# Eight gate products emitted ahead of the layer norm that follows the convolution

## The chip, the cores and the metric

The kernel runs on one core of one Trainium2 chip. The metric is the device time of one execution in microseconds (us); of several runs the median is compared.

## The reference, cut to what matters

Three transformer blocks follow one another over 512 tokens of width 1024. The change lies in the first. Its convolution branch gates a product, convolves it over 31 taps, normalizes the result over the channels and projects it; a second gate, `g_conv`, is a product of the block's normed input `h` with 1024 columns of `w_in` and needs nothing of the convolution:

```python
(q, kc, vc, ks_, vs_, kw, vw, g_nsa, u_a, u_b, g_attn, g_conv) = jnp.split(rms_norm(x) @ w_in, ...)
z = u_a * sigmoid(u_b)
z = depthwise_conv(z, conv_w) + conv_b                    # 31 taps
zn = (z - mean(z)) * rsqrt(var(z) + EPS) * ln_g + ln_b    # over the channels
conv = silu(zn) @ w_conv_out + b_conv_out
merged = sigmoid(g_attn) * attn + sigmoid(g_conv) * conv
x = x + merged @ w_out
```

## The kernel before, in words

All activations lie transposed in SBUF: 8 tiles of 128 channels by 512 tokens (`X[:, k]`, k = 0 to 7). A product ("gemm", L165 to L174) makes one 128x512 tile of its result: it takes a weight unit of 128x1024, which SP's queue loads into one of two raw buffers (`wst`), ACT rounds in two halves to `wh` (L155) and POOL completes with the rest `wl` (L156); `wh` and `wl` have four half-unit buffers each, so two units. TensorE (PE) then runs 24 matmuls, for each of 8 input tiles one each of L171, L172 and L173, into one PSUM bank (`pg`). The eviction of the gates is done by `proj` (L675 to L683): DVE multiplies `pg` by the root-mean-square factor `R` (L680).

The convolution of a channel tile is 30 DVE instructions over one PSUM bank `py` (L673), with ACT's first tap ahead of them (L671) and ACT's copy into `X[:, c]` behind them (L674). They are emitted in the attention stage, but with their place put back by 3000:

```python
with tc.high_priority(offset=-LOW):      # LOW = 3000
    y = K.ps("y")
```

The order of instructions on each engine is not the order of the source. A planner (the Tile scheduler) lays it out before the kernel runs: it reckons through the program with costs of its own, and whenever an engine is free in that reckoning it takes, of the instructions that it reckons ready, the one emitted first. What stands on an engine's list is then executed in that order, whatever becomes ready earlier on the chip; a list's head that waits holds up all behind it. The planner also reckons when a buffer is free. Behind the attention stage the PSUM pool is closed and a new one of eight banks is opened (`K.psum(g=5, m=3)`): five banks for products, three for column sums.

After that come, in this order of emission:

- `norm.feed(k)`, k = 0 to 7 (L286 to L303): a first column sum on PE over tiles 0 and 1 (`colsum`, L198, one fp32 matmul with a matrix of ones, two rows in the trace) gives `c`, which ACT copies (L295); DVE subtracts `c` from each tile (L306), ACT squares it (L314), DVE adds up sums and squares (L277).
- at k = 7 `finish` (L317 to L333): two more column sums, mean `mu` (L321), variance, then `newton` (L212 to L224): a preload of an ACT table (L209), Ln (L216), Exp (L217), three DVE steps that end with `r` (L224). While they go on, `mu` is subtracted, four tiles on DVE and four on POOL (L331).
- the eight gate products: `proj(I["w1_gc"][m])` and ACT's tanh into `gc` (L1015).
- for each tile: multiply by `r` (DVE L336), ACT affine (L1021), ACT tanh (L1023), DVE L1024, and the split into two operands `zn` (DVE L193, L194).
- the eight products of the convolution branch's projection, which read `zn` (`w1_co`), each ended by ACT L1030 and DVE L1031, L1032 (with `gc` and the attention) and the split `mg`; then the eight products of `w_out`, which read `mg`.

Of the kernel before, what the change touches and what calls it, by code (L numbers as in the profile page):

```python
# [21 lines left out]
NT = 8  # L22
# [568 lines left out]
def block1(K, X, entry):  # L591
# [84 lines left out]
    def proj(w, scale=None, out=None):  # L676
        ps = K.gemm(K.gps(), gx, w if isinstance(w, list) else K.wunit(w))
        s = K.tmp() if out is None else out
        if scale is None:
            nc.vector.tensor_tensor(s, ps, R, MUL)  # L680
        else:
            nc.vector.scalar_tensor_tensor(s, ps, scale, R, op0=MUL, op1=MUL)
        return s  # L683
# [323 lines left out]
    sC = ExitStack()  # L1007
    norm = Norm(0, K, X, 1e-6, sC)
    pC = sC.enter_context(tc.tile_pool(name="b1d", reuse_waits="tile", bufs=16))
    for k in range(NT):  # L1010
        norm.feed(k)
    sgc = []
    for m in range(NT):
        sgc.append(pC.tile([P, T], F32, tag="gc", bufs=8, name=K.nm("gc")))
        nc.scalar.activation(sgc[m], proj(I["w1_gc"][m]), AF.Tanh, scale=0.5)  # L1015
    zn = []
    alloc = lambda tag: (lambda: pC.tile([P, T], F32R, tag=tag, name=K.nm(tag)))
    for k in range(NT):
# [1016 lines left out]
def program(tc, I, out, first=1, last=3):  # L2035
    with ExitStack() as es:
# [7 lines left out]
        if first == 1:  # L2044
            block1(K, X, entry)
        else:
            tc.nc.sync.dma_start(X, I["x_in"].rearrange("(c p) t -> p c t", p=P))
            K.psum(g=5, m=3)
# [36 lines left out]
```

## Time and profile before

| | us |
|---|---|
| median of 3 runs | 2914.58 (2907.49 to 2914.98) |
| the profiled execution | 2904.16 |
| its span in the trace | 2902.4 |

The span runs from the first to the last instruction that the profiler recorded; the rest of the profiled execution, 1.8 us, lies around it. All times of the trace are counted from the span's start. The stage that the change touches lies at 487 to 620 us.

### The profile page before, as it was taken

The numbers are of one execution on the slowest core, as the hardware profiler recorded it, in microseconds if no ns is written. First come the engines' busy times: TensorE is split into PE (matmuls) and PEld (weight loads), VectorE is DVE, ScalarE is ACT, GpSimd is POOL, SyncE is SP. The second block draws the span as 40 slices with busy tenths as digits, with TensorE's granted clock in tenths as the row PEclk, the third lists the DMA queues.
The fourth block names the chain that finished last, engine by engine and source line by source line (L and its number), as shares of the span: only waits on it lengthen the run. The fifth ranks groups of instructions, "written<-read, shape, count | busy, mean of one in ns | idle before, by whom it ended". The sixth has DMA issues, their size and how long they took to land.

```text
span 2902.4 us, 34153 instructions
## 1 busy us (share of the span) xinstructions
PE 2676.3 (92%) x12206; PEld 2120.0 (73%) x12206; DVE 1780.9 (61%) x2825; ACT 1283.2 (44%) x2317; POOL 1306.6 (45%) x1023
## 2 busy tenths in 40 slices
PE   7899999699999988988889999999988889999997
PEld 5677776478888856766676788877766678788885
DVE  7889899965243596776774821126877765422246
ACT  4357875533222354444443533332556652322234
POOL 6554432554444454333332644454544344444443
PEclk9999999799999999999999999999999899999999
DMA  3321111232322222222222222232222122222223
GB/s 115 114 86 54 54 38 37 77 105 91 98 95 94 95 67 96 70 78 73 70 70 68 67 101 95 95 116 88 94 89 75 49 80 87 92 98 95 95 95 102
DMA packets 79193, 243.32 MB, mean 84 GB/s; under 512 B 11312, under 2 KB 15320, under 8 KB 79024
## 3 DMA queue, kind: packets, MB, share of 16 engines
q1 hardware_dynamic: 79024, 241.15, 25.3%
q8 instruction: 96, 1.57, 0.2%
q14 instruction: 73, 0.60, 0.1%
HBM read 230.96 MB, written 4.52 MB: 81 GB/s over the span
## 4 chain that ended last, share of the span: by engine, by line
PE 63%; DVE 23%; ACT 6%; DMA 3%; issue 3%; POOL 2%; SPq 0%; DVEq 0%; ACTq 0%; POOLq 0%
PE pg L172 18%; PE pg L173 18%; PE pg L171 18%; DMA B<-diag 2%; DVE p L1894 1%; DVE py L673 1%; DVE X L336 1%; DVE QK L1310 1%; PE ppt L956 1%; POOL wl L156 1%; DMA diag<-dg 1%; DVE ln L277 1%; DVE Zt L1416 1%; PE ps L934 1%; DVE Z L1417 1%
## 5 line engine op out<-in xcount | busy, mean ns | idle before, releaser
L156 POOL TENSOR_TENSOR wl<-wst,wh 128x512 fp32r<-128x512 f32 (+1 forms) x808 | 1099.9, 1367 | 1367.1 <-ACT wh L155 1285.7
L155 ACT ACTIVATE wh<-wst 128x512 fp32r<-128x512 f32 (+1 forms) x808 | 500.8, 627 | 1102.1 <-PE pg L172 918.1
L171 PE MATMUL pg<-op,wh 128*128 128x512 f32 (+1 forms) x2008 | 812.7, 405 | 38.9 <-ACT wh L155 19.5
L172 PE MATMUL pg<-op,wh 128*128 128x512 f32 (+1 forms) x2008 | 808.6, 403 | 2.6 <-DVE op L191 2.4
L173 PE MATMUL pg<-op,wl 128*128 128x512 f32 (+1 forms) x2008 | 807.2, 402 | 3.9 <-POOL wl L156 3.9
L171 PEld LDWEIGHTS pg<-op,wh 128*128 128x128 f32 (+1 forms) x2008 | 386.7, 193 | 120.9 <-ACT wh L155 20.1
L173 PEld LDWEIGHTS pg<-op,wl 128*128 128x128 f32 (+1 forms) x2008 | 386.2, 192 | 83.6 <-POOL wl L156 6.7
L172 PEld LDWEIGHTS pg<-op,wh 128*128 128x128 f32 (+1 forms) x2008 | 387.3, 193 | 82.2 <-DVE op L191 5.8
L171 PE MATMUL pg<-hid,wh 128*128 128x512 f32 x688 | 272.2, 396 | 0.9 <-DVE hid L190 0.9
L173 PE MATMUL pg<-hid,wl 128*128 128x512 f32 x688 | 272.1, 396 | 0.0
L172 PE MATMUL pg<-hid,wh 128*128 128x512 f32 x688 | 271.8, 395 | 0.2 <-DVE hid L191 0.2
L673 DVE SCALAR_TENSOR_TENSOR py<-z,vec,py 128x512 f32<-128x512 f32 x240 | 180.2, 751 | 10.9 <-ACT py L671 6.2
L1120 DVE TENSOR_TENSOR X<-X,pg 128x512 f32<-128x512 f32 x56 | 38.5, 688 | 222.1 <-PE pg L173 222.1
L171 PEld LDWEIGHTS pg<-hid,wh 128*128 128x128 f32 x688 | 129.2, 188 | 32.9 <-DVE hid L190 1.3
L172 PEld LDWEIGHTS pg<-hid,wh 128*128 128x128 f32 x688 | 129.2, 188 | 31.9 <-DVE hid L191 0.5
L173 PEld LDWEIGHTS pg<-hid,wl 128*128 128x128 f32 x688 | 129.2, 188 | 31.3 <-issue 0.2
L190 DVE CAST hid<-t 128x512 fp32r<-128x512 f32 x86 | 53.0, 616 | 145.7 <-ACT t L1097 145.0
L1111 DVE SCALAR_TENSOR_TENSOR t<-pg,R 128x512 f32<-128x512 f32 x32 | 22.1, 691 | 84.0 <-PE pg L173 83.9
L938 ACT ACTIVATE P<-ps,s 128x128 f32<-128x128 f32 (+3 forms) x128 | 66.4, 523 | 11.6 <-DVE s L937 9.5
L191 DVE TENSOR_TENSOR hid<-t,hid 128x512 fp32r<-128x512 f32 x86 | 63.6, 740 | 3.0
L937 DVE TENSOR_REDUCE s<-ps 128x1 f32<-128x128 f32 (+3 forms) x128 | 60.1, 483 | 8.1 <-PE ps L936 6.6
L960 DVE TENSOR_TENSOR PTl<-ppt,PTh 128x512 fp32r<-128x512 f32 x80 | 53.4, 684 | 4.7 <-ACT PTh L959 3.9
(523 smaller groups left out, 4344.3 us busy)
## 6 DMA issues: line engine op xcount, KB each, us to landing
wst<-in_w_f_dram SPq DMA_DIRECT2D x64, 512.0 KB
wst<-in_w_up_dram SPq DMA_DIRECT2D x32, 512.0 KB
wst<-in_w_down_dram SPq DMA_DIRECT2D x32, 512.0 KB
wst<-in_w_ga_dram SPq DMA_DIRECT2D x24, 512.0 KB
wst<-in_w_fg_dram SPq DMA_DIRECT2D x22, 512.0 KB
wst<-in_w_fu_dram SPq DMA_DIRECT2D x22, 512.0 KB
wst<-in_w_q_dram SPq DMA_DIRECT2D x16, 512.0 KB
wst<-in_w_out_dram SPq DMA_DIRECT2D x16, 512.0 KB
```

Source lines behind the costliest of these rows:

```text
L155: nc.scalar.activation(h, st, AF.Copy)
L156: nc.gpsimd.tensor_tensor(l, st, h, SUB)
L171: self.nc.tensor.matmul(ps, lhsT=wh, rhs=h[:, sl], start=first and k == 0, stop=False)
L172: self.nc.tensor.matmul(ps, lhsT=wh, rhs=l[:, sl], start=False, stop=False)
L173: self.nc.tensor.matmul(ps, lhsT=wl, rhs=h[:, sl], start=False, stop=last and k == n - 1)
L190: nc.vector.tensor_copy(h, src)
L191: nc.vector.tensor_tensor(l, src, h, SUB)
L673: nc.vector.scalar_tensor_tensor(y, z[:, k:k + T], w(k), y, op0=MUL, op1=ADD)
L937: nc.vector.tensor_reduce(mx[:, h:h + 1], S[:, :L], AX, MAX, negate=True)
L938: nc.scalar.activation(Pt[h][:, :L], S[:, :L], AF.Exp, bias=mx[:, h:h + 1], accum_out=den[:, h:h + 1])
L960: nc.vector.tensor_tensor(tl, pt, th, SUB)
L1120: nc.vector.tensor_tensor(X[:, m], X[:, m], ps, ADD)
```

## The change

The loop that feeds the layer norm and the loop that emits the eight gate products trade places. No instruction is added, removed or altered; a product's loads, roundings, matmuls, eviction and tanh move with it.

```diff
     norm = Norm(0, K, X, 1e-6, sC)
     pC = sC.enter_context(tc.tile_pool(name="b1d", reuse_waits="tile", bufs=16))
-    for k in range(NT):
-        norm.feed(k)
+
     sgc = []
     for m in range(NT):
         sgc.append(pC.tile([P, T], F32, tag="gc", bufs=8, name=K.nm("gc")))
         nc.scalar.activation(sgc[m], proj(I["w1_gc"][m]), AF.Tanh, scale=0.5)
+    for k in range(NT):
+        norm.feed(k)
     zn = []
```

## Rows read from the trace of the kernel before

**Rows 1.** The page's head: span, and PE's busy time, share and instructions.
```profile
span 2902.4 us, 34153 instructions
PE 2676.3 (92%) x12206; PEld 2120.0 (73%) x12206; DVE 1780.9 (61%) x2825; ACT 1283.2 (44%) x2317; POOL 1306.6 (45%) x1023
```
**Rows 2.** Stretches of the stage: length, busy us of each engine, clock, DMA share, GB/s.
```profile
487.10:504.30 17.20, 14.82 (x51) 11.07 (x50) 14.95 (x22) 1.97 (x3) 0.00 (x0) 0.80 0.03 10
504.30:523.10 18.80, 0.06 (x2) 0.04 (x1) 17.01 (x25) 2.93 (x6) 0.01 (x1) 0.63 0.00 0
523.10:537.70 14.60, 7.36 (x14) 3.88 (x14) 13.64 (x20) 5.52 (x10) 10.32 (x4) 0.50 0.11 36
537.70:573.90 36.20, 33.97 (x138) 27.04 (x137) 34.54 (x40) 26.61 (x39) 23.81 (x15) 0.92 0.33 103
573.90:620.30 46.40, 46.34 (x199) 37.01 (x198) 34.49 (x38) 16.85 (x28) 25.20 (x18) 1.00 0.37 125
```
**Rows 3.** Timeline of PE: start, length, line, operation, idle time before and its releaser.
```profile
489.49 2.05 PE L198 MATMUL pm<-ln,ones 128*128 128x512 f32 x2 [2.38 <-DVE ln L292]
...
490.55 1.42 PE L171 MATMUL pg<-op,wh 128*128 128x512 f32 x1
...
503.94 0.39 PE L173 MATMUL pg<-op,wl 128*128 128x512 f32 x1
523.06 0.79 PE L171 MATMUL pg<-op,wh 128*128 128x512 f32 x1 [18.74 <-ACT wh L155]
...
524.82 0.80 PE L173 MATMUL pg<-op,wl 128*128 128x512 f32 x1 [0.54 <-POOL wl L156]
...
534.88 3.78 PE L198 MATMUL pm<-ln,ones 128*128 128x512 f32 x4 [6.71 <-DVE ln L277]
...
573.89 0.40 PE L171 MATMUL pg<-zn,wh 128*128 128x512 f32 x1
...
619.01 0.40 PE L171 MATMUL pg<-mg,wh 128*128 128x512 f32 x1
...
997.92 1.12 PE L198 MATMUL pm<-ln,ones 128*128 128x512 f32 x2
```
**Rows 4.** Timeline of ACT around the end of the convolution.
```profile
518.81 0.60 ACT L674 ACTIVATE X<-py 128x512 f32<-128x512 f32 x1 [23.78 <-DVE py L673]
519.31 0.59 ACT L295 ACTIVATE c<-pm 128x512 f32<-128x512 f32 x1
...
522.40 0.61 ACT L155 ACTIVATE wh<-wst 128x512 fp32r<-128x512 f32 x1
```
**Rows 5.** Timeline of DVE.
```profile
484.60 0.68 DVE L680 TENSOR_TENSOR t<-pg,R 128x512 f32<-128x512 f32 x1
...
535.36 0.68 DVE L680 TENSOR_TENSOR t<-pg,R 128x512 f32<-128x512 f32 x1
...
549.89 8.02 DVE L336 TENSOR_TENSOR X<-X,r 128x512 f32<-128x512 f32 x6
...
561.06 0.68 DVE L336 TENSOR_TENSOR X<-X,r 128x512 f32<-128x512 f32 x1
561.66 0.68 DVE L194 SCALAR_TENSOR_TENSOR zn<-X,zn 128x512 fp32r<-128x512 f32 x1
562.26 0.41 DVE L193 TENSOR_SCALAR zn<-X 128x512 fp32r<-128x512 f32 x1
...
577.52 1.67 DVE L194 SCALAR_TENSOR_TENSOR zn<-X,zn 128x512 fp32r<-128x512 f32 x1
```
**Rows 6.** Timeline of ACT: table loads before Ln and Exp; below, the next norm.
```profile
542.80 1.28 ACT L216 ACT_TABLE_LOAD   x1 [1.16 <-DVE ln L326]
544.10 0.63 ACT L216 ACTIVATE ln<-ln 128x512 f32<-128x512 f32 x1
...
545.27 1.28 ACT L217 ACT_TABLE_LOAD   x1
...
1046.04 0.63 ACT L217 ACTIVATE r<-ln 128x512 f32<-128x512 f32 x1
```

## The prediction

> **What bounds the kernel now.** The page's head first: PE is busy 92% of the span [rows 1], so most of the kernel pays for a stall only where PE itself stalls. The table of stretches then shows where this stage is different: from 504.3 to 523.1 us PE does next to nothing while DVE is busy 17.0 of 18.8 us, from 523.1 to 537.7 PE runs at a granted clock of 0.50, the lower of its two levels (1.2 of 2.4 GHz), and only in the last stretch, at 1.00, is it full [rows 2]. PE's timeline names the holes: 18.74 us before a matmul of a gate product that waits for ACT's `wh`, and 6.71 us before the column sums that wait for DVE [rows 3]. ACT's timeline says why `wh` is late: ACT sits 23.78 us before the copy L674, because DVE still works on the taps of the convolution's last tile; `c` and then `wh` stand behind that copy on ACT's list [rows 4]. So the stage is a chain: taps, `c`, feed, column sums, `r`, apply, `zn`, and then eight products of `zn` that fill PE from 573.89 to 619.01. The gate products fill holes of this chain: two run while the taps go on (490.55 to 503.94), six beside the feed and the apply.
>
> **What order the planner will give.** This decides the case, and the trace of before tells how the planner reckons. The first two gate products are through on PE by 504.2, but the first of their evictions stands at 535.36 on DVE's list, behind all the taps and the whole feed [rows 3, 5]. The taps are put back by 3000 places; had the planner reckoned a product done while taps were left, it would have put the eviction among them, as it did at 484.60 with an eviction of the attention stage [rows 5]. So in its reckoning the new PSUM banks open only when the taps' accumulator is given back, that is at the copy L674. The same shows on ACT: the split of the third unit, which needs the first product to free a buffer, stands behind L674 and `c` [rows 4]. At that moment the planner has both the first column sum and the gate products ready; before, the column sum was emitted first and PE's list begins with it (489.49 [rows 3]). After the change the products are emitted first. Their weights come two units ahead, and a unit costs ACT two splits and POOL two differences (0.61 us for one split [rows 4]) against 5.6 us of PE for a product (24 at 46.40/199 = 0.233 us [rows 2]); so I see no gap in the planner's run of products into which the column sum would be let. I take it that PE's list becomes: eight gate products, then the first column sum, and all the rest of the norm behind it.
>
> **The change part by part.** No work is removed or added. What moves, with each effect:
>
> 1. The first two products go ahead of the first column sum. They gain some 3 us on the chip, worth nothing: the third needs `wh`, which stays behind L674 on ACT's list.
> 2. Products three to eight. ACT starts `wh` in the place where `c` is now, at 519.31; PE follows 0.66 us later, as 523.06 follows 522.40 [rows 3, 4]: 519.97. 144 matmuls by 0.233 us are 33.6 us. The pause before them costs a slow start: after the pause before 490.55, 48 took 503.94 + 0.23 - 490.55 = 13.6 us instead of 11.2, so 2.4 us; and 0.5 us for the first `wl` [rows 3]. They end at 556.5.
> 3. The first column sum, 1.12 us at the full clock [rows 3], brings `c` to 557.6 instead of 519.31: 38.3 us late. In the meantime DVE has only six evictions to do. This is the price: behind that column sum wait `c` on ACT and the whole feed on DVE, and nothing else is ready to fill DVE.
> 4. Feed. From `c` to the column sums it takes 534.88 - 519.31 = 15.6 us now. POOL's weight splits, busy 10.3 us beside it [rows 2], fall away; I allow 1 us for that: 572.2.
> 5. Column sums to the first L336, 549.89 - 534.88 = 15.0 us now. Two table loads of 1.28 us each stand in this chain, because a gate's tanh lies between the preload and Ln [rows 6]; with all tanhs done before, Exp follows without a load, as at the next norm [rows 6]. With 2.6 us of loads and one eviction of 0.7 us gone it is 11.7 us: 583.9.
>    The Trainium skill ("ScalarE: Activation LUTs", What ACT_TABLE_LOAD costs) puts a drain of about 1.38 us beside each load. Here Ln starts 1.30 us after its load does [rows 6], no drain to be seen; by the page's figure the two loads would be worth 5.3 us, and the sum would come out 2.7 us lower.
> 6. Apply. Six L336 take 8.02 us while POOL splits gate weights, 1.34 us each; one alone is followed by the next instruction after 0.60 us [rows 5]. Gate weights are done by then, so 8 tiles by three steps of 0.60 us and one of 0.41 us are 17.7 us, against 579.2 (577.52 and its 1.67) - 549.9 = 29.3 us now. The first `zn`, which now comes 12.4 us after the first L336 (562.34), should come after some 6: 589.9; the last at 601.6.
> 7. The eight products of `zn`. Now 619.01 - 573.89 = 45.1 us, begun when the gate products end. After the change PE is free long before, and starts with the first `zn`, slowly at first (2.4 us as above): 589.9 + 45.1 + 2.4 = 637.4. The `zn` still to come don't hold it: by 601.6 it can do at most some 45 matmuls, and two units of weights offer 42 before the last `zn`.
>
> Sum: 637.4 - 619.0 = 18.4 us later, and all behind it on PE moves with it. On the profiled execution's 2904.16 us (span 2902.4 and 1.8 around it) that is 2922.6. This execution lies 10.4 us under the median of the runs, 2914.58, and the forecast for the median is 2933.0.
>
> Bounds. The least: no slow start in 2 and 7 (4.8 us) and 1.6 us more saved in the feed, +12 us. The most: none of the savings of steps 4 to 6, first `zn` at 562.3 + 38.3 = 600.6, and 47.5 us behind it, 648.1 or +29 us. The own range of this case is 2926 to 2944. A difference of 0.3% (8.7 us) is about what a measurement of this kernel can tell from no change.
>
> **The rivals.**
>
> *The holes are filled and nothing is pushed back* (faster). If the planner finds the weights of the third product not ready and lets the first column sum in behind the second, `c` stays at 519 to 521, the feed runs as now, and the six products run beside it from 520, done at about 559. The `zn` chain, less 3.3 us of step 5, ends at 576; 42 matmuls of the `zn` products are then done, 150 by 0.233 us are 35.0: 611, 8 us sooner, 2906.6. For it speak PE's holes, 18.74 and 6.71 us; against it the reckoning above. It decides at one place: whether a column sum stands on PE's list ahead of the third product. This is also what the Trainium skill ("Perfetto Trace Analysis", Optimization Strategies) would lead one to expect, which says to keep the matmul engine as busy as possible; here the question is what the work put into the holes pushes aside.
>
> *The change does little* (same). The column sum slips in between later products, say behind the fourth: `c` is then about 16 us late (519.97 + 11.2 + 2.9 + 1.1 = 535.2), of which steps 4 to 6 give back 4.3 us plus part of the apply's 11.6; since now 11.5 us pass between the first `zn` (562.34) and its first product (573.89), the rest is mostly slack. Or the list comes out as before. Either way 2910 to 2919.
>
> **How the numbers follow.** Pushed back: 0.78. Little or nothing: 0.12. Filled: 0.10. The time predicted is the first case's, 2933. The range reaches from 2910, which takes in most of the case without effect, up to the first case's upper bound, 2944. The filled case lies at -8 us, just inside 0.3%, but grows by some us if the apply also loses part of its slow L336: of its 0.10, 0.07 go to faster and 0.03 to same, which with the second rival's 0.12 gets 0.15; slower gets 0.78.
>
> **What the profile would show.** Right: on PE 192 matmuls of gate products in one row ahead of the first L198 of this norm, that L198 at 555 to 559; DVE mostly idle from 520 to 557; no table load right before Ln or Exp; L336 near 0.68 us; PE idle some 30 us from 558, then the first product of `zn` near 590 and the first of `mg` near 637. Wrong: an L198 ahead of the third gate product, or `c` near 520. Then the time is not later but sooner. What would leave the mechanism but change the size: an apply that is as slow as now, or products of `zn` that wait for each `zn` in turn.

## The result and the profile after

The kernel after takes 2929.32 us (median of five runs, 2923.55 to 2931.89); the kernel before has a median of 2911.11 us beside it, also of five (2906.87 to 2914.98). The ratio is 1.0061, 95% interval 1.0048 to 1.0073: the change makes the kernel 18.2 us slower.

The profiled execution of after took 2929.32 us as well, with a span of 2927.5 us. PE does the same work (the page's head, against [rows 1]), and ACT runs three instructions fewer, three table loads (74 in the trace, 77 before):

```profile
span 2927.5 us, 34154 instructions
PE 2676.7 (91%) x12206; PEld 2120.6 (72%) x12206; DVE 1772.4 (61%) x2825; ACT 1280.6 (44%) x2314; POOL 1297.4 (44%) x1023
```

The span is 25.1 us longer than before's 2902.4, but not all of that belongs to the change. The stage's clock starts at the copy L674 of the last tile (518.81 us before [rows 4], 524.08 after) and ends at the first matmul of `mg` (619.01 before [rows 3], 640.18 after). So 5.3 us of the difference were there when the stage began; the stage itself grew from 100.20 to 116.10 us, by 15.9; and 2927.5 - 640.18 = 2287.3 us follow it against 2283.4, 3.9 us more. The 5.3 and the 3.9 us come and go between executions: over the ten traces of this case the last product of attention with the split `PTl` (L963) starts at 485.9 to 492.9 us, and 2283 to 2291 us follow the stage, in no order that goes with the kernels.

The timeline of PE in after (start, length, line, operation, idle time before it and its releaser) answers [rows 3]:

```profile
491.40 0.50 PE L963 MATMUL po<-PTl,VS 128*128 128x512 f32 x1 [0.23 <-DVE PTl L960]
...
525.25 0.79 PE L171 MATMUL pg<-op,wh 128*128 128x512 f32 x1 [21.98 <-ACT wh L155]
...
559.70 0.40 PE L173 MATMUL pg<-op,wl 128*128 128x512 f32 x1
559.94 1.02 PE L198 MATMUL pm<-ln,ones 128*128 128x512 f32 x2
574.96 3.75 PE L198 MATMUL pm<-ln,ones 128*128 128x512 f32 x4 [14.00 <-DVE ln L277]
591.75 1.19 PE L171 MATMUL pg<-zn,wh 128*128 128x512 f32 x2 [13.04 <-ACT X L1022]
...
640.18 0.39 PE L171 MATMUL pg<-mg,wh 128*128 128x512 f32 x1
```

No column sum stands between the third product and 559.94. PE's holes have not gone away, they have moved: 6.71 us before the column sums became 14.00, and 13.04 us before the `zn` products are new. The timeline of ACT shows `wh` in the place behind the copy that `c` had [rows 4], and Ln and Exp without the table loads of [rows 6]:

```profile
524.08 0.60 ACT L674 ACTIVATE X<-py 128x512 f32<-128x512 f32 x1 [23.78 <-DVE py L673]
524.58 1.14 ACT L155 ACTIVATE wh<-wst 128x512 fp32r<-128x512 f32 x2
...
561.47 0.58 ACT L295 ACTIVATE c<-pm 128x512 f32<-128x512 f32 x1
...
583.30 0.63 ACT L216 ACTIVATE ln<-ln 128x512 f32<-128x512 f32 x1 [3.54 <-DVE ln L326]
583.96 0.63 ACT L217 ACTIVATE r<-ln 128x512 f32<-128x512 f32 x1
```

The stretches of the stage in after (start:end, length; busy us of PE, PEld, DVE, ACT, POOL with instructions; clock, DMA share, GB/s), against [rows 2]:

```profile
506.40:525.25 18.85, 0.00 (x1) 0.00 (x1) 18.05 (x25) 1.17 (x3) 0.00 (x0) 0.55 0.00 0
525.25:559.94 34.69, 34.55 (x145) 28.03 (x146) 3.46 (x5) 12.67 (x21) 19.26 (x15) 0.95 0.32 106
559.94:574.96 15.02, 1.02 (x4) 0.23 (x2) 13.57 (x23) 6.65 (x11) 1.26 (x1) 0.71 0.11 35
574.96:591.75 16.79, 3.75 (x5) 1.17 (x5) 15.03 (x20) 8.52 (x12) 6.45 (x4) 0.50 0.00 0
591.75:640.18 48.43, 47.71 (x192) 37.51 (x193) 43.43 (x52) 19.38 (x32) 22.81 (x15) 0.95 0.38 120
```

Read DVE down the third number: while PE runs six products, DVE is busy 3.5 of 34.7 us. Then DVE works and PE is idle. What ran side by side before runs one after the other.

### The profile page after: what moved, and what is told of

The parts are those of the page before. It is cut to its first block, busy times and chain, and to the rows that moved or that the text cites. A ratio compares the mean times of both kernels' runs of the same rounds, so it can differ in the third digit from the quotient of the medians.

```text
span 2927.5 us, 34154 instructions
## 1 busy us (share of the span) xinstructions
PE 2676.7 (91%) x12206; PEld 2120.6 (72%) x12206; DVE 1772.4 (61%) x2825; ACT 1280.6 (44%) x2314; POOL 1297.4 (44%) x1023
## 4 chain that ended last, share of the span: by engine, by line
PE 64%; DVE 20%; ACT 6%; issue 4%; DMA 3%; POOL 2%; SPq 0%; DVEq 0%; ACTq 0%; POOLq 0%
PE pg L172 18%; PE pg L173 18%; PE pg L171 18%; DMA B<-diag 2%; DVE p L1895 1%; DVE QK L1311 1%; PE ppt L956 1%; DMA diag<-dg 1%; POOL wl L156 1%; PE ps L934 1%; DVE Zt L1417 1%; DVE ln L277 1%; DVE Z L1418 1%; PE po L962 1%; ACT wh L155 1%
## 5 line engine op out<-in xcount | busy, mean ns | idle before, releaser
L171 PE MATMUL pg<-op,wh 128*128 128x512 f32 (+1 forms) x2008 | 810.5, 404 | 43.2 <-ACT wh L155 23.3
L171 PEld LDWEIGHTS pg<-op,wh 128*128 128x128 f32 (+1 forms) x2008 | 386.0, 192 | 124.8 <-ACT wh L155 23.9
L171 PE MATMUL pg<-hid,wh 128*128 128x512 f32 x688 | 272.2, 396 | 0.8 <-DVE hid L190 0.8
L673 DVE SCALAR_TENSOR_TENSOR py<-z,vec,py 128x512 f32<-128x512 f32 x240 | 180.3, 751 | 10.9 <-ACT py L671 6.2
L171 PEld LDWEIGHTS pg<-hid,wh 128*128 128x128 f32 x688 | 129.2, 188 | 32.6 <-DVE hid L190 1.2
L190 DVE CAST hid<-t 128x512 fp32r<-128x512 f32 x86 | 51.9, 603 | 145.7 <-ACT t L1098 144.9
L938 ACT ACTIVATE P<-ps,s 128x128 f32<-128x128 f32 (+3 forms) x128 | 66.4, 523 | 11.7 <-DVE s L937 9.7
L960 DVE TENSOR_TENSOR PTl<-ppt,PTh 128x512 fp32r<-128x512 f32 x80 | 53.5, 685 | 4.6 <-ACT PTh L959 3.7
```

The lines of the kernel that those rows point to most:

```text
L171: self.nc.tensor.matmul(ps, lhsT=wh, rhs=h[:, sl], start=first and k == 0, stop=False)
L190: nc.vector.tensor_copy(h, src)
L673: nc.vector.scalar_tensor_tensor(y, z[:, k:k + T], w(k), y, op0=MUL, op1=ADD)
L938: nc.scalar.activation(Pt[h][:, :L], S[:, :L], AF.Exp, bias=mx[:, h:h + 1], accum_out=den[:, h:h + 1])
L960: nc.vector.tensor_tensor(tl, pt, th, SUB)
```

## The experiments

Two things had to be told apart: whether the price is the wait of the chain behind the products (theory), or something that each moved product costs; and why the products don't run during the taps. All stages below run from that last L963 (L968 or L970 in kernels with lines added) to the first matmul of `mg`; it is called the end of attention, though two small matmuls follow it, and is used since some of the kernels move L674 itself. In before that row is

```profile
486.15 0.50 PE L963 MATMUL po<-PTl,VS 128*128 128x512 f32 x1 [0.23 <-DVE PTl L960]
```

| kernel | stage us | against before | `c` after L674 | kernel, ratio to before (95%) | in us |
|---|---|---|---|---|---|
| before | 132.86 | | 0.50 | | |
| after | 148.78 | +15.9 | 37.39 | 1.0061 (1.0048 to 1.0073) | +18.2 |
| ahead2 | 132.72 | -0.1 | 3.61 | 1.0005 (0.9992 to 1.0018) | +0.6 |
| ahead4 | 135.17 | +2.3 | 15.94 | 1.0022 (1.0012 to 1.0031) | +7.0 |
| ahead6 | 144.36 | +11.5 | 26.90 | 1.0043 (1.0026 to 1.0059) | +10.8 |
| e1_colsum_first | 138.91 | +6.1 | 0.49 | 1.0033 (1.0021 to 1.0045) | +9.9 |
| m2 | 132.92 | +0.1 | 0.50 | 1.0003 (0.9991 to 1.0015) | +1.5 |
| y_before | 121.99 | -10.9 | before it | 0.9968 (0.9956 to 0.9980) | -9.3 |
| y_after | 124.44 | -8.4 | 6.40 | 0.9978 (0.9969 to 0.9988) | -5.4 |
| y_defer | 124.35 | -8.5 | before it | 0.9978 (0.9967 to 0.9989) | -7.8 |

The ratio is the recorded one and the last column the difference of two medians, so the two can be a us or two apart. The stage is the finer measure, as far as one trace of each kernel tells: m2, where nothing should change, is 0.1 us from before, and from the end of attention to L674 it takes 32.66 to 32.68 us in all seven kernels that leave the accumulator where it was.

### How the price grows with the products moved

The three kernels ahead2, ahead4 and ahead6 put the feed behind the second, fourth and sixth product:

```diff
     for m in range(NT):
+        if m == 4:
+            for k in range(NT):
+                norm.feed(k)
         sgc.append(pC.tile([P, T], F32, tag="gc", bufs=8, name=K.nm("gc")))
         nc.scalar.activation(sgc[m], proj(I["w1_gc"][m]), AF.Tanh, scale=0.5)
-    for k in range(NT):
-        norm.feed(k)
```

ahead2: 

> Two of the eight gate products are emitted ahead of the feed, six behind it. The stage is measured from the copy L674 of the last tile to the first matmul of mg, 100.2 us before. Theory (the price is the wait of the first column sum behind the products, less the chain's slack): the two products run during the taps and are through long before L674, so the column sum behind them is not late and the feed stays as before: stage 99 to 102 us, kernel within 3 us of before. Rival (2.0 us for each product moved): stage 104 us, kernel +4 us.

ahead4: 

> Four of the eight gate products are emitted ahead of the feed, four behind it. Theory (the chain is pushed back by the products that stand ahead of the first column sum on PE, less the slack that it has): two products run during the taps, the third and fourth take some 13 to 14 us behind the wait for wh, so c comes about 16 us after the copy L674 instead of 0.5 us. The chain had 11.5 us of slack before the change (first zn 562.34, its first product 573.89), and gets some more from gates that are done sooner. The stage comes to 100 to 105 us against 100.2 before, the kernel to 0 to +5 us. Rival (the cost is proportional to the products moved, as it would be if each moved product itself cost time, by its clock, its loads or its eviction): 15.9 us / 8 = 2.0 us each, stage 108 us, kernel +8 us.

ahead6: 

> Six of the eight gate products are emitted ahead of the feed, two behind it. Theory: four products behind L674 make c about 26 us late, and only some 16 us of it are slack or given back by the faster feed and apply: with the measured 2.3 us for four ahead (c 15.4 us late) and 15.9 us for eight (36.9 us late), the stage comes to 107 to 110 us (+7 to +10), the kernel to +8 to +12 us. Between four and eight the price grows with c, at 0.6 to 1.0 us for each us that c is late, below four not. Rival (2.0 us for each product moved): stage 112 us, kernel +12 us.

Measured: -0.1, +2.3 and +11.5 us of stage, where a price of 2.0 us for each product would have given +4, +8 and +12. Six alone could be either, as its 111.7 us from L674 are 2 us over what the theory gave; two and four are against the rival. But ahead2 came to its number by another way than the theory's, for its feed does not stay as before. In the timeline of PE of ahead2

```profile
497.90 1.02 PE L198 MATMUL pm<-ln,ones 128*128 128x512 f32 x2
520.03 0.79 PE L171 MATMUL pg<-op,wh 128*128 128x512 f32 x1 [21.11 <-ACT wh L155]
...
542.00 3.75 PE L198 MATMUL pm<-ln,ones 128*128 128x512 f32 x4 [4.51 <-DVE ln L277]
...
565.30 0.50 PE L171 MATMUL pg<-zn,wh 128*128 128x512 f32 x1
...
569.79 0.50 PE L173 MATMUL pg<-zn,wl 128*128 128x512 f32 x1 [3.71 <-POOL wl L156]
```

the later column sums come 55.8 us behind the end of attention (486.19), 7.1 us later than in before; the first `zn` product comes at 79.1 us, 8.6 us sooner, and the eight of them take 53.6 us instead of 45.1, 6.1 us of it waits for weights and for `zn`, at a granted clock of 0.97 over the eight against 1.00 [rows 2].

What the stages have in common is PE's idle time. The matmuls of the stage are the same in all five kernels; PE's waits between them add up to 30.6 us in before, 31.7 in ahead2, 35.3 in ahead4, 45.4 in ahead6 and 49.7 in after, and the rest of the stage, in which PE works, is 102.3, 101.0, 99.9, 98.9 and 99.0 us. So the 15.9 us of after are 19.1 us more of idle time, less 3.2 us that the matmuls take less (the six products had a granted clock of 0.95, where in before the first of them began at 0.50 [rows 2]).

In the timeline of PE of ahead4

```profile
535.45 1.02 PE L198 MATMUL pm<-ln,ones 128*128 128x512 f32 x2
552.60 2.56 PE L198 MATMUL pm<-ln,ones 128*128 128x512 f32 x4 [2.28 <-DVE ln L277]
...
574.89 1.19 PE L171 MATMUL pg<-zn,wh 128*128 128x512 f32 x2 [10.75 <-DVE zn L193]
...
623.46 0.39 PE L171 MATMUL pg<-mg,wh 128*128 128x512 f32 x1
```

the column sum lets `c` go 15.4 us later than in before, and still the first `zn` product starts no later: 86.6 us behind the end of attention (488.29), against 573.89 - 486.15 = 87.7 in before. Of these, 11.5 us were the slack between the first `zn` and its product; the apply gives some 4.5 more, as from the first L336 to that product it takes 7.9 us now, where before the first `zn` alone took 12.4. The 2.3 us come after that product has started, since PE starts the `zn` products out of a hole of 10.75 us and needs 48.6 us for them instead of 45.1. Six products use the slack up, and their feed is slower as well: there `c` to column sums takes 17.8 us (546.79 to 564.62) where all eight ahead leave 13.5. The 4.3 us are four L277 steps of 1.75 to 1.77 us, each beside a weight split on POOL; in after every one of them takes 0.69 or 0.70, and POOL splits nothing meanwhile. So a us of lateness has no one price: from 3.6 to 15.9 us late it costs 2.4, from 15.9 to 26.9 it costs 9.2, from 26.9 to 37.4 another 4.4.

The kernel's time of ahead4 (+7.0, interval +3.5 to +9.0) is above its stage, by 1 us over the interval's edge; what the rest is, its trace doesn't tell.

### Only the first column sum brought forward

The first column sum and `c` are cut out of `norm.feed` into `norm.begin` and emitted ahead of the products; all else is as in after:

```diff
+    norm.begin()
     sgc = []
     for m in range(NT):
```

> The kernel after, with one piece moved back: the first column sum and ACT's copy of it (c) are emitted ahead of the gate products, the rest of the feed and the two later column sums stay behind them. The stage is measured from the copy L674 of the last tile to the first matmul of mg: 100.2 us before, 116.1 after. Theory (what is emitted behind the products goes behind them on PE's list, and each column sum that PE's list holds back is a wait of the chain): c comes back to right behind L674, as before, and the feed on DVE runs beside the products; but the two later column sums still stand behind all eight products, about 36 us after L674, where the feed would have let them go 16 us after it. From there on 12.0 + 65.2 - 12.0 us as after (column sums to the first L336 12.0 us, column sums to mg 65.2 us): 36 + 65 = 101 us, so the stage ends about 15 us sooner than after, and the kernel lies at +1 us (-2 to +4) against before. Rival 1 (the place of the first column sum is nothing, the cost comes from the products standing ahead of the later two): the stage stays near 116, the kernel near +16 to +18. Rival 2 (the cost is not in the order but in work that meets elsewhere, as DVE's or POOL's): no change of the stage either, with c early and the column sums late.

Of the 15.9 us, 9.9 are given back: DVE is busy 19.7 of the 38.0 us in which PE runs the six products, where it was 3.5 of 34.7. What is left is the second half of the theory, that the two later column sums stand behind all eight products. The last step of the feed in the timeline of DVE:

```profile
540.40 0.69 DVE L277 TENSOR_TENSOR ln<-ln,ln 128x512 f32<-128x512 f32 x1
```

So the feed is done at 541.1. The timeline of PE has them 21.5 us later, right behind the last product:

```profile
524.60 0.80 PE L171 MATMUL pg<-op,wh 128*128 128x512 f32 x1 [18.78 <-ACT wh L155]
...
562.64 1.88 PE L198 MATMUL pm<-ln,ones 128*128 128x512 f32 x4
...
578.48 1.19 PE L171 MATMUL pg<-zn,wh 128*128 128x512 f32 x2 [13.96 <-ACT X L1027]
```

The column sums come 42.3 us behind the copy (520.35), not 36: the products start 3.1 us later, as `c` and the first steps of the feed are again ahead of `wh` on ACT's list, and need 38.0 us instead of 34.7. In the end the stage was 5 us longer than I had worked out, since I had left out what the feed, back beside the products, costs them. Rival 1 is out (6.1, not 16), and so is rival 2.

### The accumulator of the taps in a pool of its own

The prediction read from the lists that the products can't go on during the taps because the planner opens the new PSUM banks only when the old pool's last buffer, the accumulator `y`, is given back. In y_before and y_after it gets a pool of one bank that is opened ahead of the attention's pool and kept through the convolution branch; the new pool then has one bank fewer for column sums. y_before has before's order of emission, y_after that of after.

```diff
-    K.psum(g=2, s=2, pt=2, o=1, y=1)
+    K.yst = ExitStack()
+    K.yp = K.yst.enter_context(tc.tile_pool(name="psy", bufs=1, space=PSUM, reuse_waits="tile"))
+    K.psum(g=2, s=2, pt=2, o=1)
...
-            y = K.ps("y")
+            y = K.yp.tile([P, T], F32, tag="y", name=K.nm("py"))
...
-    K.psum(g=5, m=3)
+    K.psum(g=5, m=2)
```

The kernel m2 has the last of these edits alone.

y_before: 

> The kernel before, with the accumulator of the taps in a PSUM pool of its own (one bank, held until the taps are through) and two banks for column sums in the new pool instead of three. The order of emission is that of before. Theory (the products wait for the taps only because the planner opens the new banks when the last buffer of the old pool, the taps' accumulator, is given back): with the accumulator elsewhere the new banks open when the attention ends, so the splits wh stand ahead of L674 on ACT's list, the evictions of gate products stand among the taps, and PE's hole of 18.7 us before the third product is gone. Six products of 5.6 us, slowed by the lower clock, then run from about 504 to 540; the norm's chain keeps its start at L674 and meets fewer gate splits and tanhs on ACT, POOL and DVE. The chain from L674 as in the kernel after (13.5 us feed, 12.0 to the first L336, 4.8 to the first zn product, 48.4 for the eight: 79 us, from c) gives a stage of about 80 to 90 us, but the evictions between the taps delay L674 itself by up to 6 times 0.7 us = 4 us. The kernel lies at -6 to -16 us. Rival (the products are held by something else, the weights' buffers or their loads): hole and time as before, within 3 us.

y_after: 

> The kernel after (products emitted ahead of the feed), with the accumulator of the taps in a PSUM pool of its own and two banks for column sums, as in the run before this one. Theory (the change costs time only because the products cannot go on during the taps): they now run from 487 on through the taps, eight at 5.6 to 6.5 us, and end at about 535, 16 us behind L674 instead of 36. The first column sum follows at once, and the stage is about 20 us shorter than after's 116, 92 to 100 us: the kernel lies at -8 to 0 us against before, some us behind the run with before's order. Rival (what costs is the order by itself, wherever the banks are): the stage stays near 116 us and the kernel at +16.

m2: 

> The kernel before with two banks for column sums in the new pool instead of three, and nothing else: the part of the runs with a separate accumulator that is not the accumulator. Theory (the separate pool alone made those runs faster): the stage stays at 99 to 102 us, the kernel within 3 us of before. Rival (the number of column-sum banks matters, since a third is not held up for one of them): stage 5 us or more away from 100.2, in the direction of the runs with two banks, that is some 10 us less.

m2 changes nothing, so the third bank is no part of it. The accumulator is. In y_after (its L203, L176, L681 are L198, L171, L674 of before) the timeline of PE shows no wait between the end of attention and the first column sum:

```profile
485.88 0.50 PE L970 MATMUL po<-PTl,VS 128*128 128x512 f32 x1 [0.22 <-DVE PTl L967]
...
530.22 1.02 PE L203 MATMUL pm<-ln,ones 128*128 128x512 f32 x2
545.25 3.75 PE L203 MATMUL pm<-ln,ones 128*128 128x512 f32 x4 [14.00 <-DVE ln L282]
561.95 1.22 PE L176 MATMUL pg<-zn,wh 128*128 128x512 f32 x2 [12.95 <-DVE zn L198]
...
610.32 0.39 PE L176 MATMUL pg<-mg,wh 128*128 128x512 f32 x1
```

All eight products are through by 530, 4.9 us behind the copy (525.35) instead of 35.9. From the column sum on, the chain takes what it takes in after: 80.1 us to `mg` (610.32 - 530.22) against 80.2 (640.18 - 559.94). The chain is the same and stands 24.2 us earlier, counted from the end of attention (44.3 us behind it against 68.5). With the accumulator apart, the same change of order costs 2.5 us of stage (124.44 against 121.99) instead of 15.9. The kernel's -5.4 us are within what was expected, and the stage from L674 is 85.0 us, shorter than the 92 to 100: the products end earlier than the 535 I had, and L674 itself comes 6.8 us later than in after (39.5 us behind the end of attention), with evictions among the taps.

y_before has the shortest stage and the lowest median, 2897.73 us against 2906.98 of before. PE's hole of 18.74 us is gone; what is left are waits of the chain, in the timeline of PE:

```profile
545.80 3.78 PE L203 MATMUL pm<-ln,ones 128*128 128x512 f32 x4 [9.41 <-DVE ln L282]
...
562.62 1.19 PE L176 MATMUL pg<-zn,wh 128*128 128x512 f32 x2 [13.04 <-ACT X L1028]
```

So the rival of this run, that weights or loads hold the products, is out. Of the 10.9 us, 5.7 are idle time of PE (24.9 against 30.6) and 5.2 are less time for the same matmuls. Its DVE timeline shows evictions (L687) among the taps (L680) and the feed (L282, L311) ahead of the last ones:

```profile
506.50 1.78 DVE L282 TENSOR_TENSOR ln<-ln,ln 128x512 f32<-128x512 f32 x1
508.21 1.28 DVE L687 TENSOR_TENSOR t<-pg,R 128x512 f32<-128x512 f32 x2
...
514.94 3.92 DVE L680 SCALAR_TENSOR_TENSOR py<-z,vec,py 128x512 f32<-128x512 f32 x5
518.76 0.68 DVE L687 TENSOR_TENSOR t<-pg,R 128x512 f32<-128x512 f32 x1
...
544.32 0.69 DVE L311 TENSOR_TENSOR X<-X,c 128x512 f32<-128x512 f32 x1 [2.90 <-ACT X L681]
```

Here my picture of how it would come about was wrong, and the time right. I had the copy 4 us late at most and the feed behind it; it came 54.7 us behind the end of attention instead of 32.7, because the feed of the tiles that were done, and evictions, went ahead of the last tile's taps. For the chain that is as good: only one tile's share of the feed is left behind the copy, and the two column sums follow it after 2.1 us.

### The copy freed of what stands ahead of it

The 2.90 us of the last line above are seven tanhs (3.75 us) that stand ahead of the copy on ACT. In y_defer, which is y_before otherwise, the evictions go into the gates' own buffers, and the tanhs are put back like the taps:

```diff
-        nc.scalar.activation(sgc[m], proj(I["w1_gc"][m]), AF.Tanh, scale=0.5)
+        proj(I["w1_gc"][m], out=sgc[m])
+        with tc.high_priority(offset=-LOW):
+            nc.scalar.activation(sgc[m], sgc[m], AF.Tanh, scale=0.5)
```

> As the run y_before (before's order, accumulator in a pool of its own), but each gate's eviction goes into the gate's own buffer and its tanh is put back by 3000 places like the taps. In y_before the copy L674 of the last tile stood 3.7 us behind seven tanhs on ACT and six evictions of 0.6 us stood among the taps on DVE. Theory: five products run during the taps into the five banks, the last three behind L674; the copy comes about 7 us sooner (536 to 537 instead of 543.7 us), the two later column sums at about 540 instead of 545.8, the last three products fill PE's hole before the zn products until about 560, and the first matmul of mg comes at 604 to 608 instead of 611.0. Kernel: -12 to -16 us against before. Rival (PE now sets the end, since three products follow the copy at the lower clock): the zn products start at 563 or later and nothing is gained over y_before, -9 us.

The copy came 5.9 us sooner (48.8 us behind the end of attention), the column sums 5.4 us sooner (51.4 against 56.75), and the stage ended 2.4 us later than in y_before: nothing gained. The rival has the result but not the reason: the `zn` products start 72.4 us behind the end of attention, 1.2 us sooner than in y_before, and what they wait for is `zn`, not PE. In the DVE timeline of y_defer

```profile
547.80 1.78 DVE L227 SCALAR_TENSOR_TENSOR ln<-ln,r 128x512 f32<-128x512 f32 x1
549.50 0.68 DVE L687 TENSOR_TENSOR gc<-pg,R 128x512 f32<-128x512 f32 x1
550.10 1.33 DVE L228 TENSOR_TENSOR ln<-ln,r 128x512 f32<-128x512 f32 x1
551.46 1.81 DVE L229 SCALAR_TENSOR_TENSOR r<-ln,r 128x512 f32<-128x512 f32 x1
```

the last three steps of `r` take 1.78, 1.33 and 1.81 us, where each took 0.69 in y_after, and an eviction stands among them; POOL splits weights of the last products meanwhile (wl of 1.74, 1.30 and 1.29 us at 547.29, 549.58, 551.44). From column sums to the first `zn` product y_defer needs 21.1 us, y_before 16.8, and the `zn` products then take 51.9 us instead of 48.4, with waits of 0.2 to 0.9 us for `zn`. The three products left beside the chain take back what the early copy gives. That POOL's work is what stretches the three steps is read from their standing side by side, as for the feed of ahead6, and was not tried by itself.

## Why the prediction held, step by step

The order, which decided the sign, came out as forecast: products, first column sum, the rest; and its reason, the release of the accumulator, is borne out by y_before and y_after: with the accumulator apart the products go on during the taps, and evictions stand among them. That it is the release of the buffer, and not the shared pool in some other way, is read from the lists. The stage grew by 15.9 us where the sum had 18.4. Term by term, from L674:

- *Products (steps 1 and 2).* To their end 35.9 us, forecast 37.7. PE took up 1.17 us behind the copy, as said; the 34.7 us from there hold 1.1 us over the bare 33.6, not 2.9: the slow start of the clock was over-priced, and 0.95 was granted over this stretch.
- *`c` (step 3).* 37.4 us behind the copy, forecast 38.8. "Nothing else is ready to fill DVE" is the 3.46 us of the second stretch.
- *Feed (step 4).* 13.5 us, forecast 14.6: I allowed 1 us for the weight splits that fall away, it was 2.1. In before two steps of the feed, beside weight splits on POOL (523.09 to 526.45), take 1.76 us; in after, without splits beside it, all such steps take 0.69 or 0.70. The timeline of DVE in before:

```profile
523.55 1.76 DVE L277 TENSOR_TENSOR ln<-ln,X 128x512 f32<-128x512 f32 x1
525.24 1.76 DVE L277 TENSOR_TENSOR ln<-ln,ln 128x512 f32<-128x512 f32 x1
```

- *Column sums to L336 (step 5).* 12.0 us, forecast 11.7, with no table load in between. The reason given holds for Ln: in before a gate's tanh loads its own table at 539.71, between the preload and Ln's load. Exp loads again, though only a weight split stands between Ln and it; in after, where nothing comes between the preload and Ln, neither loads. The 2.6 us go by the loads' own length; in ahead4, where a tanh stands between preload and Ln again, Ln starts 1.30 us after its load, as in [rows 6]:

```profile
559.17 1.28 ACT L216 ACT_TABLE_LOAD   x1 [0.79 <-DVE ln L326]
560.47 0.63 ACT L216 ACTIVATE ln<-ln 128x512 f32<-128x512 f32 x1
```

  The drain that the Trainium skill puts beside each load ("ScalarE: Activation LUTs", What ACT_TABLE_LOAD costs) is not to be seen there either, and the step came out by the row's price, not by the page's.
- *Apply and `zn` products (steps 6 and 7).* 53.2 us from the first L336 to `mg`, forecast 53.5. The two parts erred against each other a little: first `zn` product 4.8 us behind L336, forecast 6 to the `zn`, and 48.4 us of products, forecast 47.5. The last `zn` came 20.1 us behind the first L336, not 17.7: ACT's last two tiles stand behind weight splits, and DVE waits. Step 7's count of the matmuls that PE could do by then was off by its own numbers (11.7 us less 2.4 of slow start, by 0.233, are 40, not 45), but it hardly matters: PE waited for a `zn` once, 0.72 us.

The timeline of DVE for the last step (five L336 in 3.10 us, against six in 8.02 [rows 5]):

```profile
586.96 3.10 DVE L336 TENSOR_TENSOR X<-X,r 128x512 f32<-128x512 f32 x5
...
602.27 1.80 DVE L1025 SCALAR_TENSOR_TENSOR X<-ln,X 128x512 f32<-128x512 f32 x1 [1.17 <-ACT ln L1024]
...
606.36 0.69 DVE L194 SCALAR_TENSOR_TENSOR zn<-X,zn 128x512 fp32r<-128x512 f32 x1
```

Together -1.4 - 1.1 + 0.3 - 0.3 = -2.5 us. That the kernel's +18.2 us nonetheless stand so near the 18.4 is in part luck: 2.3 us of them lie outside the stage, where two executions can differ by 7 to 8 us. The forecast of 2933.0 stood on a median of 2914.58; the median beside after's runs was 2911.11.

The rivals: "filled and nothing pushed back" would have needed a column sum ahead of the third product, and e1_colsum_first shows that even then the later two hold the end 6 us back. ahead2 comes nearest to the list that this rival supposes (497.90 against 520.03), and there, too, the 8 us are not gained: the 8.6 us by which the first `zn` product comes sooner are lost again within the eight of them. "Little" needed it behind the fourth, and ahead4 shows that this is a stage of +2.3 us, as the slack of 11.5 us was read.

## What to carry to other kernels

Before work is moved into an engine's hole, look at what then stands behind it on that engine's list: a 1 us column sum at the head of a chain is worth more than 34 us of products that nobody waits for yet. Find out why the hole is there: here it was one accumulator that in the planner's reckoning held back the new pool's banks, and taking it out of their pool gave more (10.9 us of stage) than any order of emission that was tried. Where a kernel's time varies by several us, measure the stage between two fixed instructions; here the same row of work repeated to 0.2 us from kernel to kernel. And count the idle time of the engine that sets the end: a change that fills one hole and opens another, as ahead2 does, has gained nothing.

## What the runs showed that was not expected

- Slack ends abruptly. The same chain was 15 us late for 2.3 us and 26 us late for 11.5.
- Taking 5.9 us out of the copy's wait moved the end by +2.4 us (y_defer): three steps of 0.69 us became 1.3 to 1.8 us beside POOL's weight splits.
- A slow start of PE has no one price: after a hole of 22 us with a clock of 0.55, six products ran at 0.95 and lost 1.1 us; after waits of 14.0 and 13.0 us the eight `zn` products ran at 0.95 as well, and lost 2.6 us beside their wait of 0.72.
